# Attention scores of an encoder block: the products with the queries' lo parts in half the array's rows, side by side, with the stages of a unit in another order

## The chip, the core and the metric

The kernel runs on one core of a Trainium2 chip. The metric is the device time of one execution in microseconds; the time before is the median of three runs. The engines are named as in the profile: PE (TensorE, matrix multiplication; PEld is its loading of weights), DVE (VectorE), ACT (ScalarE), POOL (GpSimd), SP (SyncE, which here only issues transfers).

## What is computed

One encoder block on 2048 positions of 1024 channels in float32: an input projection, four heads of differential attention beside Fourier mixing, an output projection, a gated MLP with a convolution of width three, and norms. The change concerns attention. Each head has two components of queries and keys (64 channels each) and one set of values (128 channels):

```
s = jnp.einsum('bqhcd,bkhcd->bhcqk', qi, k) * scale
s = s - slopes[None, :, None, None, None] * dist[None, None, None]
p = jax.nn.softmax(s, axis=-1)
a = p[:, :, 0] - lam * p[:, :, 1]
return jnp.einsum('bhqk,bkhv->bqhv', a.astype(v.dtype), v)
```

The index `c` is the component, and `dist` the distance of the two positions. The output of a head is then normalized (its scale goes into the output projection).

## The kernel before

**Precision.** The matmuls' operands have the type float32r. Each is split (`split`, lines 77 to 87) into a hi part, a copy converted to float32r (ACT), and a lo part, the difference (DVE mostly). A product is the sum of three matmuls, hi by hi, hi by lo and lo by hi (`mm3`, lines 119 to 128).

**Where queries and keys come from.** `in_proj` writes them, split, to DRAM: `qd` and `kd` are indexed by head, component, hi or lo, channel (64) and position (lines 272 to 275). Queries carry the factor of the scores already.

**A unit of attention** is one head and one block of 128 queries, so there are 4 x 16 = 64 units, heads outside. The loop of lines 657 to 686 goes in steps, four to a unit; `t` counts them, and step `t` serves several units at different stages:

- `scores(n, c, half)`, lines 543 to 577: the scores of unit n for component c against 1024 keys, one call a step. The 64 channels of a component leave half of PE's 128 rows over, so the keys' hi and lo parts are stacked: a key tile has, for each component, hi in partitions 0 to 63 and lo in 64 to 127 (`load_k`). The query tile holds four blocks (component, hi or lo), each one twice, in the upper and the lower 64 partitions (`load_q`). So a matmul with the hi query gives hi by hi plus hi by lo, and one with the lo query gives lo by hi plus lo by lo: two matmuls for each 512 keys, four a call, 16 a unit, all with 128 rows (line 567). They go into a PSUM tile `s` of 128 x 1024; there are two of these. A DVE pass (line 572) adds the distances, writes the result to the unit's tile `z` and keeps a running minimum. After the second half, ACT computes the exponential of the 128 x 2048 tile and its sum (line 576).
- `combine(n, half)`, lines 579 to 589: DVE makes the coefficient of the second component from the two sums (lines 583 and 585); POOL, with ACT for a quarter of the columns, scales the second component by it (`scale_half`, lines 439 to 444) and POOL adds it to the first (line 589).
- `transposes(n, g)`, lines 591 to 600: two units later, four of the 16 key blocks a step are transposed on PE into one of two PSUM tiles `pt` (line 598), and split into the tile `at` by ACT (hi, line 81) and DVE (lo, line 82).
- `values(pr, kbs)`, lines 602 to 609: products with the values for a pair of units, two key blocks a step, six matmuls of 256 columns, into a PSUM tile `o`.
- `finish(pr, stage)`, lines 611 to 632: squares and copy out of PSUM on ACT, sums of squares on PE (line 624), and the norm's scale in four small POOL instructions (lines 628 and 630 to 632).

In the loop, a unit n issues in its own four steps the scores of component 0 in steps 0 and 1 and of component 1 in steps 2 and 3, with the exponentials at steps 1 and 3; the first half of combine comes in step 3 and the second in step 0 of the next unit. `zp` has three tiles `z` for each component.

**What orders the work.** Each engine works through a queue in order. The queues' order comes from the framework in which the kernel is written: it takes the order of issue as a priority and moves instructions by a model of when they are ready, so a queue can differ from the order of the code. Loads of queries, keys and values are issued from POOL: two issues for a query tile of 512 positions (line 504, every four units) and two for a head's keys (line 458).

**Around it.** The first units of attention are issued among the last steps of the Fourier mixing (`fourier`); the output projection follows.

Of the kernel before, what the change touches and what calls it, by code (L numbers as in the profile page):

```python
# [20 lines left out]
P = 128  # L21
D = 1024
S = 2048
NB = S // P
KB = D // P
H = 4
DH = 64
# [3 lines left out]
HALF = 512  # L31
# [4 lines left out]
SLOPES = [2.0 ** (-8.0 * (h + 1) / H) for h in range(H)]  # L36
# [4 lines left out]
class Block:  # L41
# [96 lines left out]
    def in_proj(self, es_u, es_f):  # L138
        nc, a = self.nc, self.a
        up = self.pool(es_u, "u", 1, side="right")  # L140
        self.up = up
        with ExitStack() as es, ExitStack() as es01:
# [47 lines left out]
            with ExitStack() as esn:  # L190
# [15 lines left out]
                for _ in range(20):  # L206
                    r = nc.tensor.transpose(busy[:, :P], self.ident, self.ident)
# [3 lines left out]
                u = [up.tile([P, HALF], F32, tag="u", bufs=18, name=f"u{n}") for n in range(NB)]  # L211
                r = {}
# [37 lines left out]
            for blk, b, gs in ((1, 0, range(4)), (1, 1, range(4)), (0, 0, (0, 1)), (0, 1, (0, 1)),  # L250
                               (0, 1, (2,)), (0, 0, (2, 3)), (0, 1, (3,))):
                dst = self.kd if blk else self.qd
                if (blk, b, gs) == (0, 1, (2,)):
                    es01.close()
                    self.fourier_operands(es_f, pst)
                else:
                    wt = weights(blk * HALF + b * W)
                for g in gs:
                    row = p.tile([P, HALF], F32, tag="row", name=f"row{blk}{b}{g}")
                    nc.sync.dma_start(row, self.rsd[g * HALF:(g + 1) * HALF].partition_broadcast(P))  # L260
                    for hh in range(2):
                        h, cs = 2 * b + hh, slice(hh * P, hh * P + P)
                        ps = pso.tile([P, HALF], F32, tag="o", name=f"pz{blk}_{h}_{g}")
                        self.mm3(ps, [(wt[kb][:, 0, cs], wt[kb][:, 1, cs], hth[g][:, kb, :], htl[g][:, kb, :])
                                      for kb in range(KB)])
                        st = p.tile([P, 2, HALF], F32R, tag="zst", name=f"zst{blk}_{h}_{g}")
                        z = p.tile([P, HALF], F32, tag="z", bufs=1, name=f"z{blk}_{h}_{g}")
                        nc.vector.scalar_tensor_tensor(
                            z, ps, 1.0 if blk else -1.0 / (math.sqrt(DH) * SLOPES[h]),
                            row, ALU.mult, ALU.mult)  # L270
                        self.split(z, st[:, 0, :], st[:, 1, :])
                        for c in range(2):
                            (nc.scalar if blk or gs[-1] < 3 else nc.sync).dma_start(
                                dst[h, c, :, :, g * HALF:(g + 1) * HALF].rearrange("l d t -> d l t").bitcast(F32),
                                st[c * DH:(c + 1) * DH].bitcast(F32))


# [176 lines left out]

    def load_k(self, h):
        t = self.slot(self.K_SLOT[h], [2, S], f"k{h}")
        for c in range(2):
            self.nc.gpsimd.dma_start(t[:, c], self.kd[h, c].rearrange("l d t -> (l d) t"))
        return t

    def load_v(self, h, behind=None):
# [37 lines left out]
        nc.vector.tensor_scalar(self.neglam, self.neglam, -LAMBDA_INIT, None, ALU.add)  # L499

    def load_q(self, h, n, behind=None):
        qt = self.kp.tile([P, 4, HALF], F32R, tag="q", name=f"q{h}_{n}")
        for r in range(2):
            load = self.nc.gpsimd.dma_start(
                qt[r * DH:(r + 1) * DH],
                self.qd[h].rearrange("c l d t -> d (c l) t")[:, :, n * HALF:(n + 1) * HALF])
            if behind is not None:
                self.issue_after(load, behind, True)
        return qt
# [21 lines left out]
    def attention(self, pss):  # L531

        nc, a = self.nc, self.a
        with ExitStack() as es:
# [5 lines left out]
            ks, vs, qs = {0: self.k0}, {}, {(0, 0): self.q0}  # L540
            zs, sums, recips, ats, pos = {}, {}, {}, {}, {}

            def scores(n, c, half):
                h, i = units[n]
                if c == 0 and half == 0:
                    if i % 4 == 2 and n + 2 < NU:
                        h2, i2 = units[n + 2]
                        qs[h2, i2 // 4] = self.load_q(h2, i2 // 4, self.ot_done[2] if n == 2 else None)
                    if n == 1:
                        vs[0] = self.load_v(0, self.ot_done[1])  # L550
                    kind, head = self.KV_AT.get(n, (None, None))
                    if kind == "k":
                        ks[head] = self.load_k(head)
                    if kind == "v":
                        vs[head] = self.load_v(head)
                    sums[n] = (sp.tile([P, 4], F32, tag="mn", name=f"mn{n}"), sp.tile([P, 2], F32, tag="ss", name=f"ss{n}"))
                    if n % 2 == 0:
                        recips[n // 2] = sp.tile([P, 2, 2], F32, tag="rr", name=f"rr{n}")
                mn, ss = sums[n]
                if half == 0:  # L560
                    zs[n, c] = zp.tile([P, S], F32, tag=f"z{c}", name=f"z{n}_{c}")
                zt, qt, kt = zs[n, c], qs[h, i // 4], ks[h]
                ps = pss.tile([P, 1024], F32, tag="s", name=f"s{n}_{c}{half}")
                for l in range(2):
                    for j in range(2):
                        k0 = half * 1024 + j * HALF
                        nc.tensor.matmul(ps[:, j * HALF:(j + 1) * HALF], qt[:, 2 * c + l, i % 4 * P:i % 4 * P + P],  # L567
                                         kt[:, c, k0:k0 + HALF], start=l == 0, stop=l == 1)
                d0 = (NB - 1 - i) * P + half * 1024
                m0 = c * 2 + half  # L570

                nc.vector.tensor_tensor_reduce(  # L572
                    zt[:, half * 1024:(half + 1) * 1024], ps, dist[:, d0:d0 + 1024], SLOPES[h],
                    3.0e38 if half == 0 else mn[:, m0 - 1:m0], ALU.add, ALU.min, mn[:, m0:m0 + 1])
                if half == 1:
                    nc.scalar.activation(zt, zt, AF.Exp, bias=mn[:, 2 * c + 1:2 * c + 2], scale=-1.0,  # L576
                                         accum_out=ss[:, c:c + 1])
# [79 lines left out]
            for t in range(4 * (NU + LAG + 4)):  # L657
                if t < 4 * LAG:
                    yield
                elif t == 4 * LAG:  # L660
# [7 lines left out]
                n, c, half = t // 4, t // 2 % 2, t % 2  # L668
                if n < NU:
                    scores(n, c, half)  # L670
                for args in steps.get(t, ()):
                    if args not in loading:
                        loading[args] = self.out_weights(wp, *args)
# [2 lines left out]
                for stage, lag in enumerate((8, 10)):  # L676
                    if v >= lag and (v - lag) % 8 == 0 and (v - lag) // 8 < NU // 2:
                        finish((v - lag) // 8, stage)
                if n < NU and t % 4 == 3:
                    combine(n, 0)  # L680
                if 0 <= n - LAG < NU:
                    transposes(n - LAG, t % 4)
                if 0 <= n - 1 < NU and t % 4 == 0:
                    combine(n - 1, 1)
                if 0 <= v < 8 * (NU // 2):
                    values(v // 8, [v % 8 * 2, v % 8 * 2 + 1])
# [463 lines left out]
```

## Time and profile before

| | us |
| --- | --- |
| median of three runs | 2571.42 (2570.17 to 2577.55) |
| the profiled execution's own time | 2574.7 |
| its span, first to last instruction | 2572.9 |
| attention: first and last score matmul start at | 410.3 and 954.8 |

The mean clock that PE was granted in the profiled execution was 0.992 of full speed. In the rows of the profile "L567" is line 567 of the kernel; `s<-k,q` reads "writes tile s, reads tiles k and q"; `x4` counts instructions that are shown together. A row of the chain of waits has the start, the length and the engine with tile and line. A row of the timeline has the start, the length from the first start to the last end, the engine, and in brackets how long the engine had been idle and what ended that. Matmuls are pipelined: the length shown for one is longer than the time from its start to the next one's.

### The profile page before, as it was taken

What the parts mean: (1) busy time and instruction counts of PE and PEld (TensorE: products, weight loads), DVE (VectorE), ACT (ScalarE), POOL (GpSimd) and SP (SyncE); (2) the same over time, 40 slices, a digit from 0 to 9 for tenths busy, and PEclk for the clock granted to TensorE, in tenths of its full rate; (3) what the DMA queues carried; (4) which work ended last, traced back from release to release, by engine and by line L of the source; (5) the groups of instructions that cost most, each with busy time, mean ns of one, the idle gap of its engine ahead of it and who ended that gap; (6) DMA issues with size and microseconds to landing.
All of it is one profiled execution on the core that took longest, in us unless ns stands there. A gap on an engine that the chain in (4) does not pass through costs nothing.

```text
span 2572.9 us, 34950 instructions
## 1 busy us (share of the span) xinstructions
PE 2516.6 (98%) x13021; PEld 2114.6 (82%) x13021; DVE 1752.6 (68%) x2691; ACT 1301.9 (51%) x2036; POOL 716.9 (28%) x797
## 2 busy tenths in 40 slices
PE   9999999999999999978999999999999999999998
PEld 9998877888888888866888888877888888888886
DVE  4533358988889996786877777657777777434443
ACT  6321246888888883233544454444454445333332
POOL 1300015888988883271010010000000000000000
PEclk9999999999999999988999999999999999999999
DMA  8335558343332205554222221454212222546463
GB/s 264 98 125 139 152 143 237 66 74 73 74 75 50 48 26 173 181 174 140 107 74 79 88 79 70 160 181 155 91 74 76 88 83 85 185 137 219 146 204 113
DMA packets 146154, 309.12 MB, mean 120 GB/s; under 512 B 12080, under 2 KB 69440, under 8 KB 138816
## 3 DMA queue, kind: packets, MB, share of 16 engines
q1 hardware_dynamic: 90816, 226.60, 26.2%
q0 software_dynamic: 18256, 34.57, 6.7%
q10 hardware_dynamic: 36912, 45.72, 5.8%
q8 instruction: 102, 1.67, 0.3%
q14 instruction: 68, 0.56, 0.1%
HBM read 225.05 MB, written 81.80 MB: 119 GB/s over the span
## 4 chain that ended last, share of the span: by engine, by line
PE 87%; DVE 5%; DMA 4%; issue 1%; POOL 1%; ACT 1%; SPq 0%; POOLq 0%; ACTq 0%; DVEq 0%
PE s L567 9%; PE pd L127 5%; PE pd L125 5%; PE pd L126 5%; PE pt L598 4%; PE o L125 3%; PE o L127 3%; PE o L126 3%; PE pz L125 2%; PE pz L127 2%; PE pz L126 2%; DMA hb<-htd 2%; PE pv L127 1%; PE pv L126 1%; PE pv L125 1%
## 5 line engine op out<-in xcount | busy, mean ns | idle before, releaser
L589 POOL TENSOR_TENSOR z<-z,z 128x1024 f32<-128x1024 f32 x128 | 307.1, 2414 | 0.1
L82 DVE TENSOR_TENSOR d<-wd,d 128x512 fp32r<-128x512 f32 x240 | 157.0, 689 | 211.7 <-ACT d L81 211.4
L567 PE MATMUL s<-k,q 128*128 128x512 f32 x1024 | 281.5, 396 | 3.0 <-DVE mn L572 2.0
L576 ACT ACTIVATE z<-z,mn 128x2048 f32<-128x2048 f32 x128 | 257.5, 2012 | 33.7 <-DVE mn L572 32.7
L81 ACT ACTIVATE d<-wd 128x512 fp32r<-128x512 f32 x240 | 141.8, 626 | 236.9 <-PE pd L127 186.2
L125 PE MATMUL pd<-d,d 128*128 128x512 f32 x640 | 251.8, 393 | 1.9 <-ACT d L81 1.4
L127 PE MATMUL pd<-d,d 128*128 128x512 f32 x640 | 251.2, 393 | 0.5 <-DVE d L82 0.5
L126 PE MATMUL pd<-d,d 128*128 128x512 f32 x640 | 251.5, 393 | 0.0
L567 PEld LDWEIGHTS s<-k,q 128*128 128x128 f32 x1024 | 174.5, 188 | 29.4 <-DVE mn L572 5.0
L572 DVE CUSTOM_DVE_ANT_0 z<-s,dist,mn 128x1024 f32<-128x1024 f32 x128 | 163.8, 1280 | 38.6 <-PE s L567 37.8
L82 DVE TENSOR_TENSOR at<-pt,at 128x512 fp32r<-128x512 f32 x256 | 169.9, 686 | 8.5 <-ACT at L81 8.4
L81 ACT ACTIVATE at<-pt 128x512 fp32r<-128x512 f32 x256 | 147.5, 592 | 48.2 <-PE pt L598 44.8
L125 PE MATMUL o<-at,v 128*128 128x256 f32 x512 | 162.0, 316 | 0.0
L598 PE MATMUL pt<-ident,z 128*128 128x128 f32 x1024 | 156.7, 276 | 5.1 <-DVE at L82 5.1
L572 DVE CUSTOM_DVE_ANT_0 z<-s,dist 128x1024 f32<-128x1024 f32 x128 | 155.8, 1217 | 5.4 <-PE s L567 4.4
L598 PEld LDWEIGHTS pt<-ident,z 128*128 128x128 f32 x1024 | 125.7, 144 | 36.3 <-issue 10.5
L98 POOL TENSOR_SCALAR y_rs<-y_rs 128x1 f32<-128x1 f32 x16 | 6.9, 429 | 524.9 <-ACT sq L95 524.9
L126 PE MATMUL o<-at,v 128*128 128x256 f32 x512 | 146.3, 286 | 0.0
L125 PEld LDWEIGHTS pd<-d,d 128*128 128x128 f32 x640 | 120.1, 188 | 30.6 <-ACT d L81 1.8
L127 PEld LDWEIGHTS pd<-d,d 128*128 128x128 f32 x640 | 120.1, 188 | 29.0 <-DVE d L82 1.4
L127 PE MATMUL o<-at,v 128*128 128x256 f32 x512 | 143.7, 281 | 0.0
L126 PEld LDWEIGHTS pd<-d,d 128*128 128x128 f32 x640 | 120.1, 188 | 27.7 <-DVE d L82 0.3
(1058 smaller groups left out, 6895.0 us busy)
## 6 DMA issues: line engine op xcount, KB each, us to landing
wu<-in_w_up SPq DMA_DIRECT2D x44, 1024.0 KB, 4.8
wd<-in_w_down SPq DMA_DIRECT2D x88, 512.0 KB, 3.6
wd<-gd SPq DMA_DIRECT2D x88, 256.0 KB, 3.9
q<-qd POOLq DMA_DIRECT2D x32, 512.0 KB, 7.0
gd<-t SPq DMA_DIRECT2D x22, 512.5 KB, 2.6
gd<-t SPq DMA_DIRECT2D x22, 511.5 KB, 3.1
wst<-in_w_in SPq DMA_DIRECT2D x72, 128.0 KB, 3.6
xt<-in_xt SPq DMA_DIRECT2D x16, 512.0 KB, 4.6
```

Of the source, the lines that this page charges most:

```text
L81: r = nc.scalar.activation(hi, src, AF.Copy)
L82: return r, (lo_engine or nc.vector).tensor_tensor(lo, src, hi.bitcast(F32), ALU.subtract)
L98: nc.gpsimd.tensor_scalar(t[:, 1:2], t[:, 0:1], 1.0 / D, EPS, ALU.mult, ALU.add)
L125: mm(ah, bh, start=first and i == 0, stop=False)
L126: mm(ah, bl, start=False, stop=False)
L127: r = mm(al, bh, start=False, stop=last and i == n - 1)
L567: nc.tensor.matmul(ps[:, j * HALF:(j + 1) * HALF], qt[:, 2 * c + l, i % 4 * P:i % 4 * P + P], kt[:, c, k0:k0 + HALF], start=l == 0, stop=l ...
L572: nc.vector.tensor_tensor_reduce(zt[:, half * 1024:(half + 1) * 1024], ps, dist[:, d0:d0 + 1024], SLOPES[h], 3.0e38 if half == 0 else mn[: ...
L576: nc.scalar.activation(zt, zt, AF.Exp, bias=mn[:, 2 * c + 1:2 * c + 2], scale=-1.0, accum_out=ss[:, c:c + 1])
L589: nc.gpsimd.tensor_tensor(z[:, x], z[:, x], z1[:, x], ALU.add)
L598: nc.tensor.transpose(pt[:, j * P:(j + 1) * P], zs[n, 0][:, kb * P:(kb + 1) * P], self.ident)
```

## The change

The third product pair, lo query by keys, no longer uses the whole array. Hi queries are multiplied as before with stacked hi and lo keys (128 rows). Lo queries are multiplied by hi keys alone, 64 rows: component 0 in partitions 0 to 63, component 1 in partitions 64 to 127, issued in turn, into different PSUM tiles. The product lo by lo is no longer computed. For this the keys of component 1 are stacked the other way round (lo above, hi below), so `load_k` issues three transfers a head. The query tile has three blocks instead of four (hi of each component, twice, and one block with the lo parts of component 0 above component 1), in three transfers; `qd` is indexed by hi or lo before component, so that the lo parts lie together.

One call of `scores` now makes a half (1024 keys) for both components, eight matmuls into both `s` tiles, in steps 0 and 2; the DVE passes of both follow. The exponentials are a function of their own, at steps 2 and 3, behind that step's transposes; both halves of `combine` come in step 1 of the next unit.

```diff
-                                dst[h, c, :, :, g * HALF:(g + 1) * HALF].rearrange("l d t -> d l t").bitcast(F32),
+                                d[:, :, g * HALF:(g + 1) * HALF].rearrange("l d t -> d l t").bitcast(F32),
...
     def load_k(self, h):
         t = self.slot(self.K_SLOT[h], [2, S], f"k{h}")
-        for c in range(2):
-            self.nc.gpsimd.dma_start(t[:, c], self.kd[h, c].rearrange("l d t -> (l d) t"))
+        self.nc.gpsimd.dma_start(t[:, 0], self.kd[h, 0].rearrange("l d t -> (l d) t"))
+        for l in range(2):
+            self.nc.gpsimd.dma_start(t[(1 - l) * DH:(2 - l) * DH, 1], self.kd[h, 1, l])
...
     def load_q(self, h, n, behind=None):
-        qt = self.kp.tile([P, 4, HALF], F32R, tag="q", name=f"q{h}_{n}")
-        for r in range(2):
-            load = self.nc.gpsimd.dma_start(
-                qt[r * DH:(r + 1) * DH],
-                self.qd[h].rearrange("c l d t -> d (c l) t")[:, :, n * HALF:(n + 1) * HALF])
+        qt = self.kp.tile([P, 3, HALF], F32R, tag="q", name=f"q{h}_{n}")
+        c = slice(n * HALF, (n + 1) * HALF)
+        loads = [(qt[r * DH:(r + 1) * DH, :2], self.qd[h, 0, :, :, c].rearrange("c d t -> d c t")) for r in range(2)]
+        for o, i in loads + [(qt[:, 2], self.qd[h, 1, :, :, c].rearrange("c d t -> (c d) t"))]:
+            load = self.nc.gpsimd.dma_start(o, i)
...
-            def scores(n, c, half):
+            def scores(n, half):
...
+                ps = [pss.tile([P, 1024], F32, tag="s", name=f"s{n}_{c}{half}") for c in range(2)]
+                out = lambda c, j: ps[c][:, j * HALF:(j + 1) * HALF]
+                for c in range(2):
+                    for j in range(2):
+                        nc.tensor.matmul(out(c, j), qt[:, c, u], kt[:, c, cols[j]], start=True, stop=False)
+                for j in range(2):
+                    for c in range(2):
+                        r = slice(c * DH, (c + 1) * DH)
+                        nc.tensor.matmul(out(c, j), qt[r, 2, u], kt[r, c, cols[j]], start=False, stop=True)
+                d0 = (NB - 1 - i) * P + half * 1024
+                for c in range(2):
+                    m0 = c * 2 + half
+                    nc.vector.tensor_tensor_reduce(
+                        zs[n, c][:, half * 1024:(half + 1) * 1024], ps[c], dist[:, d0:d0 + 1024], SLOPES[h],
+                        3.0e38 if half == 0 else mn[:, m0 - 1:m0], ALU.add, ALU.min, mn[:, m0:m0 + 1])
+
+            def exps(n, c):
                 mn, ss = sums[n]
...
-                for l in range(2):
-                    for j in range(2):
-                        k0 = half * 1024 + j * HALF
-                        nc.tensor.matmul(ps[:, j * HALF:(j + 1) * HALF], qt[:, 2 * c + l, i % 4 * P:i % 4 * P + P],
-                                         kt[:, c, k0:k0 + HALF], start=l == 0, stop=l == 1)
...
-                if n < NU:
-                    scores(n, c, half)
+                n = t // 4
+                if n < NU and t % 2 == 0:
+                    scores(n, t // 2 % 2)
...
-                if n < NU and t % 4 == 3:
-                    combine(n, 0)
                 if 0 <= n - LAG < NU:
                     transposes(n - LAG, t % 4)
-                if 0 <= n - 1 < NU and t % 4 == 0:
+                if n < NU and t % 4 > 1:
+                    exps(n, t % 4 - 2)
+                if 0 <= n - 1 < NU and t % 4 == 1:
+                    combine(n - 1, 0)
                     combine(n - 1, 1)
```

More of the change, by code (lines that the diff above doesn't have):

```diff
@@ L272, in in_proj @@
                         for c in range(2):
+                            d = dst[h, c] if blk else dst[h, :, c]
                             (nc.scalar if blk or gs[-1] < 3 else nc.sync).dma_start(
-                                dst[h, c, :, :, g * HALF:(g + 1) * HALF].rearrange("l d t -> d l t").bitcast(F32),
+                                d[:, :, g * HALF:(g + 1) * HALF].rearrange("l d t -> d l t").bitcast(F32),
                                 st[c * DH:(c + 1) * DH].bitcast(F32))
@@ L541, in attention @@
             zs, sums, recips, ats, pos = {}, {}, {}, {}, {}
-            def scores(n, c, half):
+            def scores(n, half):
                 h, i = units[n]
-                if c == 0 and half == 0:
+                if half == 0:
                     if i % 4 == 2 and n + 2 < NU:
@@ L558, in scores @@
                         recips[n // 2] = sp.tile([P, 2, 2], F32, tag="rr", name=f"rr{n}")
-                mn, ss = sums[n]
[L560 to L563, printed above, removed]
-                for l in range(2):
-                    for j in range(2):
-                        k0 = half * 1024 + j * HALF
-                        nc.tensor.matmul(ps[:, j * HALF:(j + 1) * HALF], qt[:, 2 * c + l, i % 4 * P:i % 4 * P + P],
-                                         kt[:, c, k0:k0 + HALF], start=l == 0, stop=l == 1)
@@ L569, in scores @@
[L569 to L577, printed above, removed]
+                    for c in range(2):
+                        zs[n, c] = zp.tile([P, S], F32, tag=f"z{c}", name=f"z{n}_{c}")
@@ new lines, in scores @@
+                mn = sums[n][0]
+                qt, kt = qs[h, i // 4], ks[h]
+                u = slice(i % 4 * P, i % 4 * P + P)
+                cols = [slice(half * 1024 + j * HALF, half * 1024 + (j + 1) * HALF) for j in range(2)]
+                ps = [pss.tile([P, 1024], F32, tag="s", name=f"s{n}_{c}{half}") for c in range(2)]
[3 more added lines that the diff above has]
+                        nc.tensor.matmul(out(c, j), qt[:, c, u], kt[:, c, cols[j]], start=True, stop=False)
@@ new lines, in scores @@
+                for j in range(2):
[3 more added lines that the diff above has]
+                d0 = (NB - 1 - i) * P + half * 1024
+                for c in range(2):
+                    m0 = c * 2 + half
+                    nc.vector.tensor_tensor_reduce(
+                        zs[n, c][:, half * 1024:(half + 1) * 1024], ps[c], dist[:, d0:d0 + 1024], SLOPES[h],
+                        3.0e38 if half == 0 else mn[:, m0 - 1:m0], ALU.add, ALU.min, mn[:, m0:m0 + 1])
@@ L579, in combine @@
+            def exps(n, c):
+                mn, ss = sums[n]
+                nc.scalar.activation(zs[n, c], zs[n, c], AF.Exp, bias=mn[:, 2 * c + 1:2 * c + 2], scale=-1.0,
+                                     accum_out=ss[:, c:c + 1])
             def combine(n, half):
@@ L667, in attention @@
                     pso = self.pool(es, "at_po", 2, PSUM)
-                n, c, half = t // 4, t // 2 % 2, t % 2
-                if n < NU:
-                    scores(n, c, half)
+                n = t // 4
+                if n < NU and t % 2 == 0:
+                    scores(n, t // 2 % 2)
                 for args in steps.get(t, ()):
```

## The prediction

> **What bounds the kernel now.** I read the page first, for the shares and the chain that ended last, then the busy time of the engines over one pair of units, then the chain inside that pair, then each engine's own queue there. The page:
>
> ```profile
> PE 2516.6 (98%) x13021; PEld 2114.6 (82%) x13021; DVE 1752.6 (68%) x2691; ACT 1301.9 (51%) x2036; POOL 716.9 (28%) x797
> ...
> PE 87%; DVE 5%; DMA 4%; issue 1%; POOL 1%; ACT 1%; SPq 0%; POOLq 0%; ACTq 0%; DVEq 0%
> ```
>
> PE (TensorE) is busy all the time and carries 87% of the chain, but these are averages over stages. The change touches attention alone, so I read that stage. The chain there, first and last regular scores and one stretch between:
>
> ```profile
> 444.78 0.93 PE s L567 x4
> ...
> 954.30 0.95 PE s L567 x4
> ```
>
> ```profile
> 649.85 0.92 PE s L567 x4
> 650.77 0.44 PE pt L598 x4
> 651.21 0.12 PE o L125
> 651.33 0.12 PE o L126
> ...
> 651.91 0.94 PE s L567 x4
> ```
>
> ```profile
> 666.92 0.93 PE s L567 x4
> ```
>
> One step is four score matmuls (0.93), four transposes (0.44) and six value matmuls (six times 0.12, 0.70), 2.07 us in all, with nothing between them. Eight steps, a pair of units, last 666.92 - 649.85 = 17.07 us, so a unit takes 8.53 us; eight times 2.07 is 16.56, and most of the rest goes to the finishing stage's matmuls (line 624). From 444.78 to 954.30 there are 509.5 / 8.53 = 59.7 units; I count 59.5, for a few small holes. What the other engines do in that pair (columns: length, then busy time of PE, weight loads, DVE, ACT, POOL, each with its count):
>
> ```profile
> 649.85:666.92 17.07, 17.07 (x117) 15.22 (x117) 15.18 (x32) 14.45 (x21) 15.02 (x14) 1.00 0.43 70
> ```
>
> PE is the bound, at full clock (1.00), but three engines are within 12 to 15% of it. This is the row that matters most: PE can give back only about a tenth before another engine is late.
>
> **The change part by part.**
>
> *The matmuls.* Every score matmul before uses the whole array. Per unit there are 16, 512 columns each; afterwards 8 whole ones and 8 of 64 rows, which are to run two at a time. One costs 0.93 / 4 = 0.235 us. If two half-row matmuls take the time of one, a unit saves 4 x 0.235 = 0.94 us; if they run one after the other it saves nothing. It cannot save more, since each still streams 512 columns. No row of before shows a matmul of fewer than 128 rows, so both ends stay. I take the full overlap: the two of a pair read different partitions, use different rows, and write different PSUM tiles, and nothing in the program orders one behind the other. The weight loads stay 16 a unit; the value matmuls above have one load each at 0.12 us, so two loads fit into the 0.235 us of a pair, just. By the Trainium skill (TensorE: Matmul & The Clock Gate, Part 3) matmuls in different row groups start some 4 ns apart, and four of 32 rows gained 3.07 times; no run here shows it yet.
>
> *The switch between whole and half rows.* Each half of a unit goes to half rows and back, four switches a unit. Nearest rows: scores to transposes costs nothing (649.85 + 0.92 = 650.77), transposes to values costs a little:
>
> ```profile
> 653.04 0.37 PE L125 MATMUL o<-at,v 128*128 128x256 f32 x1
> 653.25 0.28 PE L126 MATMUL o<-at,v 128*128 128x256 f32 x1
> 653.37 0.28 PE L127 MATMUL o<-at,v 128*128 128x256 f32 x1
> ```
>
> The first value matmul is followed after 0.21 instead of 0.12 us, so 0.09. The far end is a full wait for the matmul in flight:
>
> ```profile
> L567 PE MATMUL s<-k,q x1024: 387/395/499, 410.3 to 954.8; 128*128 128x512 f32 x171
> ```
>
> It lasts 0.395 where the next starts after 0.235, a tail of 0.16 us. So a switch costs 0 to 0.16 us, a unit 0 to 0.64; I take 0.05 a switch, 0.2 a unit, near the two cheap rows. PE's unit is then 8.53 - 0.94 + 0.2 = 7.8 us, with 7.6 and 8.25 as ends. The Trainium skill (TensorEngine Tiling (Array Packing), Key Properties) says that changing the tiling mode drains the engine. By that rule the upper end holds, and it is the third case below.
>
> *The other queues.* Their work hardly changes, so each one's own sum is a floor. DVE and ACT:
>
> ```profile
> 650.20 0.69 DVE L82 TENSOR_TENSOR at<-pt,at 128x512 fp32r<-128x512 f32 x1
> 650.81 1.28 DVE L572 CUSTOM_DVE_ANT_0 z<-s,dist,mn 128x1024 f32<-128x1024 f32 x1
> 652.02 0.09 DVE L572 DVE_READ_ACCUMULATOR2_ANT mn<- 128x1 f32 x1
> 652.02 0.69 DVE L82 TENSOR_TENSOR at<-pt,at 128x512 fp32r<-128x512 f32 x1
> 652.89 1.23 DVE L572 CUSTOM_DVE_ANT_0 z<-s,dist 128x1024 f32<-128x1024 f32 x1 [0.19 <-PE s L567]
> 654.04 0.08 DVE L572 DVE_READ_ACCUMULATOR2_ANT mn<- 128x1 f32 x1
> 654.96 1.28 DVE L572 CUSTOM_DVE_ANT_0 z<-s,dist,mn 128x1024 f32<-128x1024 f32 x1 [0.84 <-PE s L567]
> ```
>
> ```profile
> 649.60 0.57 ACT L81 ACTIVATE at<-pt 128x512 fp32r<-128x512 f32 x1
> 650.38 0.72 ACT L443 ACTIVATE z<-z,cf 128x512 f32<-128x512 f32 x1 [0.21 <-DVE cf L585]
> 651.24 0.60 ACT L81 ACTIVATE at<-pt 128x512 fp32r<-128x512 f32 x1
> 652.20 2.01 ACT L576 ACTIVATE z<-z,mn 128x2048 f32<-128x2048 f32 x1 [0.35 <-DVE mn L572]
> 654.12 0.18 ACT L576 ACTIVATION_READ_ACCUMULATOR z<-z,mn 128x1 f32 x1
> 654.21 0.57 ACT L81 ACTIVATE at<-pt 128x512 fp32r<-128x512 f32 x1
> ```
>
> From start to next start a score pass on DVE takes 1.15 (652.89 to 654.04) or 1.21 us (650.81 to 652.02), a lo split 0.6 (650.20 to 650.81): per unit 2 x 1.15 + 2 x 1.21 + 4 x 0.6 = 7.1, and with the reciprocal and its kin about 7.5 (the window's 15.18 / 2 is 7.6). ACT: 14.45 / 2 = 7.2, of which two exponentials at 2.01 each. POOL also issues the loads:
>
> ```profile
> 649.34 1.31 POOL L504 DMA_DIRECT2D q<-qd  x2
> 650.68 1.13 POOL L441 TENSOR_SCALAR z<-z,cf 128x1024 f32<-128x1024 f32 x1
> 651.78 0.19 POOL L630 TENSOR_SCALAR ft<-ft 128x2 f32<-128x2 f32 x1
> ...
> 654.97 0.71 POOL L631 TENSOR_TENSOR ft<-ft,mhalf 128x2 f32<-128x2 f32 x1
> ...
> 658.02 0.18 POOL L632 TENSOR_TENSOR fs<-ft,rr 128x2 f32<-128x2 f32 x1
> 658.18 0.19 POOL L628 TENSOR_TENSOR f<-rr 128x2 f32<-128x2 f32 x1
> 659.95 1.13 POOL L441 TENSOR_SCALAR z<-z,cf 128x1024 f32<-128x1024 f32 x1 [1.58 <-DVE cf L585]
> 661.05 0.69 POOL L444 TENSOR_SCALAR z<-z,cf 128x512 f32<-128x512 f32 x1
> 661.71 4.78 POOL L589 TENSOR_TENSOR z<-z,z 128x1024 f32<-128x1024 f32 x2
> ```
>
> A combine is 1.1 + 0.67 + 4.75 = 6.5 us, the norm 0.19 + 0.71 + 0.18 + 0.19 = 1.3 a pair, 0.65 a unit. A query load is two issues, 1.31 us, every four units; three issues afterwards, 1.95 if each costs the same; no row gives a price by size. That is 0.49 instead of 0.33 a unit. Keys go from two issues to three a head, at the same price 0.65 us in 16 units; with them and the values I add 0.1. POOL's floor becomes 6.5 + 0.65 + 0.49 + 0.1 = 7.75 us, a little above DVE's 7.5 and beside PE's 7.8. So even if everything ran packed, a unit would take about 7.75.
>
> *The stages reordered.* Now both components' score tiles of a half are filled in one step and both exponentials come ready together, instead of half a unit apart. I walk through it from the end (time 0) of the second half's scores, in the order in which the code issues; the engines' queues are sorted by a planner with costs of its own (before, ACT's queue above has hi, scale, hi, exponential, where the code issues hi, hi, scale, exponential), so this is an estimate from the rows above. With full overlap PE ends the next scores after two steps' transposes and values, 2 x 1.14, and 0.94 + 0.47, at 3.7. DVE does two passes and a lo split, to about 3.0. The first exponential starts at 1.15 + 0.18 = 1.3 (DVE's accumulator row at 652.02 to ACT's at 652.20) and holds ACT until 3.3; the transposes of the unit's last step end at about 1.6, so their hi copy waits and ends at 3.85, and the lo split behind it runs from 3.95 to 4.55: DVE stood idle for almost 1 us. Its next two passes run to 6.9 instead of 6.05. The second exponential holds ACT until 5.9, two hi copies follow to 7.0, DVE's lo splits to 8.1, and the coefficients may come ahead of the next pass too. PE meanwhile waits for the second score tile, which DVE frees at 6.9, and ends the next half at 7.85. So a unit closes at 8.1 to 8.4: DVE, held up by ACT, has taken PE's place. The planner may place a hi copy ahead of the first exponential, which pulls it towards the floor of 7.75. I take 8.2 us.
>
> *The rest.* Both halves of combine now stand one behind the other on POOL, two steps later for the first half. Ready coefficients come at about 6.2 of the walk, the first half 3.5 later, at 9.7, and the transposes that read it stand in PE's queue at about 3.7 + 8.2 = 11.9: covered, with about 2 us of slack; a query load of 1.95 in between uses it up. Two more issues ahead of the distance table at the start are 1.3 us at most, beside Fourier work. The stores of q and k keep number and size. The end of attention waits for two exponentials in a row, 1 us more. I cost these at 0 to 3 us together, and take 0.
>
> **The sum.** 59.5 units x (8.53 - 8.2) = 20 us. The profiled execution took 2574.7 (span 2572.9 and 1.8 around it), so 2554.7 against that one; the median of the three runs, 2571.42, is 3.3 lower: 2551. A difference of 0.3%, 7.7 us, is about what a measurement can tell from none.
>
> **The rivals.**
>
> *Near the floor.* The planner sorts ACT well and a unit takes 7.75 to 8.0. For it: in this pair all three helpers have over 1 us of slack a unit. Against: all four engines would be over 90% busy at once, and there are two score tiles only. 59.5 x 0.65 = 39 us less: about 2532. Chance 0.18.
>
> *Each switch drains.* PE at 8.25, and with the walk's stalls, where a wait of PE on the second score tile is no longer made up, about 8.5: 2570, no change. Chance 0.17. It is the skill's drain rule; the cheap change at 649.85 to 650.77 speaks against so high a price, though it is another kind of change.
>
> *Half-row matmuls do not overlap.* Then the change does not do what it says: PE keeps 8.53 and pays the switches, at 0.09 each 0.36 a unit: 8.9, and 59.5 x 0.36 = 21 us more, 2593. With 0.16 a switch it would be 2609. A unit has four pairs and four switches, so PE loses from the point where a pair costs more than 0.47 less one switch: with 0.09, from 0.38. Nothing in the profile speaks against it, since no row has such a matmul. Chance 0.25.
>
> **How the numbers follow.** The forecast, 2551, has 0.40 (its own range 2537 to 2566). Faster: it and the floor, 0.58; no change: the drain, 0.17; slower: 0.25. The range leaves out the best part of the floor case (below 2526) and the dearer switches (above 2594): about 2 in 10.
>
> **What would show it.** Half-row rows in the profile (64 rows of the array) at starts in pairs, a pair in about 0.24 us, and a half's scores in 1.4 to 1.5 us. A window of a pair of units of about 16.4 us instead of 17.07, PE no longer busy throughout, DVE and ACT at about 90%. Between 560 and 950 us the waits are now (total, times, longest):
>
> ```profile
> DVE z L572 <- PE s L567: 33.3, 62, 0.9
> ...
> DVE at L82 <- ACT at L81: 4.4, 19, 0.2
> ```
>
> DVE waits for PE; afterwards its lo splits should wait for ACT by tens of us, and score matmuls for DVE's passes. If PE stays at 100% of a longer pair, switches or missing overlap are the cause; if a transposition waits for POOL, its floor was set too low.

## The result, and the profile after

The time rose. The median is 2671.75 us (2666.95 to 2673.7, four runs) against 2570.8 for the kernel before beside it: a ratio of 1.0385, 95% interval 1.0362 to 1.0409, so 101 us more. The profiled execution took 2671.89 us (span 2670.1), 97 us more than the one shown of before. The forecast was 20 us less. One run of `e15_passes`, 10984 us, counts as slow and is in none of the ratios below.

The page, busy time and the chain of waits by engine:

```profile
PE 2586.3 (97%) x13021; PEld 2073.0 (78%) x13021; DVE 1760.9 (66%) x2691; ACT 1302.4 (49%) x2036; POOL 728.8 (27%) x817
...
PE 79%; DVE 7%; POOL 6%; DMA 5%; issue 3%; ACT 1%; SPq 0%; POOLq 0%; ACTq 0%; DVEq 0%
```

Two things are new at once. PE is busy for 70 us more, although a quarter of its score time was to go, and POOL has 6% of the chain instead of 1%. The groups by line show the place: the first score pass of DVE for each component, before and then after (count, shortest, median and longest length in ns, start of the first and the last):

```profile
L572 DVE CUSTOM_DVE_ANT_0 z<-s,dist x128: 1204/1216/1240, 411.9 to 953.4; 128x1024 f32<-128x1024 f32 x128
```

```profile
L583 DVE CUSTOM_DVE_ANT_0 z<-s,dist x128: 1200/1222/1256, 416.8 to 1049.6; 128x1024 f32<-128x1024 f32 x128
```

Attention starts 4.9 us later and lasts 632.8 instead of 541.5 us, 91.3 more; together 96 of the 97. Below, "a unit" is the time from DVE's first pass of unit 8 to that of unit 60, by 52: 8.55 us before, 10.23 after. Two units in the windows (length, then busy time of PE, weight loads, DVE, ACT, POOL):

```profile
699.29:719.47 20.18, 19.16 (x119) 13.70 (x118) 15.28 (x30) 14.60 (x21) 14.29 (x13) 1.00 0.03 9
```

DVE, ACT and POOL work as long as before (15.18, 14.45 and 15.02), so none of them became the bound. PE is busy for 9.6 us a unit at full clock, and 1.0 us in two units it stands still. What PE does with a half, in the chain of waits (start, length; L574 has the whole array, L578 half its rows):

```profile
706.00 0.48 PE s L574 x2
706.48 0.43 PE s L578
706.91 0.66 PE s L574 x2
707.58 0.66 PE s L578 x3
708.23 0.59 PE pt L611 x4
```

The code issues four whole and then two pairs of half-row matmuls. PE's queue has two whole, one half-row, two whole, three half-row: the planner put the parts of component 0 ahead. That is four switches a half, and one pair instead of two. Of the 128 halves 88 run like this one; 24 have two whole and two half-row matmuls twice, four switches and no pair, and 16 have the order in which the code issues. Here scores and transposes take 2.82 us, where before two steps' scores and one step's transposes took 2 x 0.93 + 0.44 = 2.30.

And where PE stands still, in the timeline (ACT, DVE, POOL and PE by turns; in brackets the idle time and what ended it):

```profile
713.81 0.19 ACT L589 ACTIVATION_READ_ACCUMULATOR z<-z,mn 128x1 f32 x1
```

```profile
717.04 0.15 DVE L596 RECIPROCAL rr<-ss 128x2 f32<-128x2 f32 x1
717.81 1.28 DVE L583 CUSTOM_DVE_ANT_0 z<-s,dist,mn 128x1024 f32<-128x1024 f32 x1 [0.62 <-PE s L578]
719.02 0.08 DVE L583 DVE_READ_ACCUMULATOR2_ANT mn<- 128x1 f32 x1
719.02 0.27 DVE L598 TENSOR_SCALAR cf<-ss,neglam,rr 128x1 f32<-128x1 f32 x1
```

```profile
719.47 1.12 POOL L442 TENSOR_SCALAR z<-z,cf 128x1024 f32<-128x1024 f32 x1 [1.99 <-DVE cf L598]
720.57 0.69 POOL L445 TENSOR_SCALAR z<-z,cf 128x512 f32<-128x512 f32 x1
721.23 4.74 POOL L602 TENSOR_TENSOR z<-z,z 128x1024 f32<-128x1024 f32 x2
```

```profile
723.65 0.65 PE L611 MATMUL pt<-ident,z 128*128 128x128 f32 x4 [1.00 <-POOL z L602]
```

A unit's sums are complete at 714.0, when ACT has its second exponential. The coefficient made of them comes only at 719.02: the last thing ahead of it in DVE's queue is a score pass of the next unit, and that pass waits for PE (0.62 us). POOL waits for the coefficient (1.99), then the transposes for POOL (1.00).

### The profile page after: what moved, and what is told of

Same layout as the page of the kernel before. It is cut to its first block, busy times and chain, and to the rows that moved or that the text cites. A ratio compares the mean times of both kernels' runs of the same rounds, so it can differ in the third digit from the quotient of the medians.

```text
span 2670.1 us, 34950 instructions
## 1 busy us (share of the span) xinstructions
PE 2586.3 (97%) x13021; PEld 2073.0 (78%) x13021; DVE 1760.9 (66%) x2691; ACT 1302.4 (49%) x2036; POOL 728.8 (27%) x817
## 4 chain that ended last, share of the span: by engine, by line
PE 79%; DVE 7%; POOL 6%; DMA 5%; issue 3%; ACT 1%; SPq 0%; POOLq 0%; ACTq 0%; DVEq 0%
PE pd L125 4%; PE pd L127 4%; PE pd L126 4%; PE s L574 4%; PE pt L611 4%; PE s L578 4%; POOL z L602 3%; PE o L125 2%; PE o L127 2%; PE o L126 2%; PE pz L125 2%; PE pz L127 2%; PE pz L126 2%; DVE z L583 2%; DMA hb<-htd 2%
## 5 line engine op out<-in xcount | busy, mean ns | idle before, releaser
L574 PE MATMUL s<-k,q 128*128 128x512 f32 x512 | 175.0, 427 | 1.0 <-DVE mn L583 0.8
L611 PEld LDWEIGHTS pt<-ident,z 128*128 128x128 f32 x1024 | 116.5, 143 | 75.7 <-POOL z L602 48.9
L578 PE MATMUL s<-k,q 64*128 64x512 f32 x512 | 156.5, 465 | 0.0
```

Source lines behind the costliest of these rows:

```text
L574: nc.tensor.matmul(out(c, j), qt[:, c, u], kt[:, c, cols[j]], start=True, stop=False)
L578: nc.tensor.matmul(out(c, j), qt[r, 2, u], kt[r, c, cols[j]], start=False, stop=True)
L611: nc.tensor.transpose(pt[:, j * P:(j + 1) * P], zs[n, 0][:, kb * P:(kb + 1) * P], self.ident)
```

## The experiments

Theory 1 (A in the expectations): the order of PE's score matmuls costs the time (switches, lost pairs). Theory 2 (B): the stages' order does, through the coefficient. Rivals were that half-row matmuls do not overlap, and that the additional transfers cost the time. All kernels (ratio and interval against the kernel before, run on the same chip):

| kernel | what | median us | ratio (95%) | unit us |
| --- | --- | --- | --- | --- |
| after | the change | 2671.75 | 1.0385 (1.0362 to 1.0409) | 10.23 |
| e1_order | half-row pairs in the written order | 2672.88 | 1.0396 (1.0377 to 1.0416) | 10.13 |
| e2_whole | stages reordered, whole array | 2624.13 | 1.0198 (1.0181 to 1.0215) | 9.37 |
| e4_stages | half rows, exps and combine at before's places | 2638.66 (one run) | | 9.42 |
| e5_both | e4 and e1 | 2644.5 | 1.0283 (1.0268 to 1.0299) | 9.69 |
| e8_coef | after, coefficient earlier | 2631.21 | 1.0229 (1.0214 to 1.0244) | 9.42 |
| e6_order_coef | e1, coefficient earlier | 2604.7 | 1.0129 (1.0113 to 1.0144) | 8.95 |
| e7_whole_coef | e2, coefficient earlier | 2593.31 | 1.0086 (1.0068 to 1.0103) | 8.88 |
| e9_serial_coef | e6, queue c0 c0 c1 c1 | 2612.99 (one run) | | 9.10 |
| e10_same_rows | e6, all half-row matmuls in the same 64 rows | 2642.84 (one run) | | 9.52 |
| e11_before_pairs | before's stages, one pair a step | 2616.19 | 1.0175 (1.0158 to 1.0192) | 9.05 |
| e12_component | a component in every second step, two pairs | 2594.62 | 1.0092 (1.0077 to 1.0107) | 8.70 |
| e13_store | e12 with before's two key transfers | 2578.67 | 1.0024 (1.0015 to 1.0034) | 8.61 |
| e14_component_whole | e13, whole array | 2586.37 | 1.0066 (1.0045 to 1.0087) | 8.74 |
| e15_passes | e13, DVE's two passes together | 2571.64 | 0.9999 (0.9990 to 1.0008) | 8.47 |
| e16_passes | e15, also lo splits ahead of the next passes | 2597.11 | 1.0097 (1.0084 to 1.0110) | 8.89 |

Slower than every range expected of them came out e1, e5, e12 and e16; e4, e6, e13, e14 and e15 fell between or just beside theirs.

**The written order alone.** `e1_order` chains the eight matmuls of a half, and nothing else:

```diff
+                for f, c, j in ((whole, 0, 0), (whole, 0, 1), (whole, 1, 0), (whole, 1, 1), (rows, 0, 0), (rows, 1, 0), (rows, 0, 1), (rows, 1, 1)):
+                    mm = f(c, j)
+                    if last is not None:
+                        self.issue_after(mm, last)
+                    last = mm
```

> The changed kernel with PE's queue held to the written order: four whole-array score matmuls, then the four half-row ones with the two components in turn, so two switches a half and two adjacent pairs, where the changed kernel's queue has four switches and one pair. From the starts in its trace a half's scores should fall from 2.3-2.4 to about 1.7 us. Theory A (the switches on PE are the whole loss): PE then has about 8.3 us of work a unit, and the time is 2550 to 2590. Theory B (the loop set by the reordered stages: coefficient behind the next unit's second-half pass on DVE, then POOL, then the transposes): a unit falls only by the scores' part of that loop, to about 9.5 us, so the time is about 2630.

The time did not move, 2672.88: theory 1 alone falls. But PE's own work did get shorter (busy 2526.7 us instead of 2586.3), and waits took its place. The chain of waits, one turn and the end of the one before it:

```profile
705.25 0.71 PE s L576 x4
705.95 1.27 DVE z L588
707.24 0.20 DVE cf L603
...
707.62 1.07 issue
708.69 0.70 POOL z L445
709.39 2.34 POOL z L607
...
711.78 0.66 PE pt L616 x4
...
714.98 0.47 PE s L572 x2
715.45 0.71 PE s L576 x4
716.15 1.27 DVE z L588
717.44 0.20 DVE cf L603
```

From coefficient to coefficient, 707.24 to 717.44, are 10.20 us, about the unit ("issue" is time in which an engine waited for nothing that the profile shows; here it is that of POOL's first scale). It is a loop: coefficient, POOL's scales and first sum, transposes, then the next scores behind them in PE's queue, DVE's pass of these scores, and behind that pass the next coefficient. Whatever PE saves in it is spent waiting for POOL (waits of e1 between 560 and 950 us: total, times, longest):

```profile
PEld pt L616 <- POOL z L607: 63.0, 31, 2.4
POOL z L442 <- DVE cf L603: 58.5, 33, 3.5
PE pt L616 <- POOL z L607: 49.5, 31, 2.0
```

**The stages alone, and the coefficient.** `e2_whole` keeps the reordered stages, with all score matmuls, loads and tiles as before:

```diff
-                        r = slice(c * DH, (c + 1) * DH)
-                        nc.tensor.matmul(out(c, j), qt[r, 2, u], kt[r, c, cols[j]], start=False, stop=True)
+                        for j in range(2):
+                            nc.tensor.matmul(out(c, j), qt[:, 2 * c + l, u], kt[:, c, cols[j]], start=l == 0, stop=l == 1)
```
 `e8_coef`, `e6_order_coef` and `e7_whole_coef` put the second-half passes of a unit behind the coefficient of the unit before in DVE's queue, on top of after, e1 and e2:

```diff
-                    nc.vector.tensor_tensor_reduce(
+                    r = nc.vector.tensor_tensor_reduce(
...
+                    if half == 1 and n > 0:
+                        self.issue_after(r, coef[n - 1])
```

> The reordered stages alone: scores of both components in one step, exponentials and combine at the new places, but all score matmuls with 128 rows as before, with the loads and tiles of before (lo by lo is computed again). Theory A: no half rows, no switches, so the time of before within 10 us, 2560 to 2580. Theory B: DVE's queue has the coefficient behind the second-half pass in every second unit, so the loop holds there; a unit of 9.0 to 9.5 us, 2600 to 2630.

> The changed kernel with the coefficient held ahead of the second-half passes and PE's queue left to the planner, which switches between whole and half rows four times a half. PE's own work is then about 9.4 us a unit (2.3 us of scores a half), and this binds: 2620 to 2640. If switches did not matter it would equal the run with the written order.

> PE's queue in the written order, and on DVE the coefficient of a unit held ahead of the next unit's second-half passes (it stood between the two). Theory B (the loop coefficient, POOL, transposes, scores, pass): POOL starts about 1.4 us earlier, the transposes' wait for it falls from 1.5-1.7 us a unit to about 0.2, and with PE's own 8.4 us a unit takes 8.5 to 8.8: 2570 to 2590. The rival, that half-row matmuls cost this time by themselves: no change from 2673.

> Whole-array score matmuls with the reordered stages (the 2624 us kernel) and the coefficient held ahead of the second-half passes. Theory B: the loop no longer binds, PE's 8.53 us does: 2575 to 2595. Against the run with half rows in written order and the same coefficient this gives what half rows are worth in themselves: by the starts in the trace 0.1 to 0.2 us a half saved, so half rows 0 to 20 us the faster.

Reordering the stages alone costs 2624.1 - 2571.0 = 53 us; with the coefficient moved, 2593.3 - 2572.2 = 21. With half rows the same move takes the 101 us to 2631.2 - 2572.2 = 59, 42 less, and the written order then takes these to 2604.7 - 2572.2 = 32.5. With the written order the same move takes 69 us, from 2672.9 - 2571.0 = 102 to 32.5. So both theories hold, but in this order: the loop first, and only without it does PE's order count, for 26.5 us where it counted for none. In `e8_coef` PE's queue mixes whole and half rows much as in the change (54 of the 128 halves like the one shown there, 35 without a pair, 39 in the written order; so the planner's order moved too, and part of the 42 us may be due to that), and it fills the chain of 700 to 722 us by itself:

```profile
by line: PE s L574 24.6%; PE s L578 23.8%; PE pt L613 17.7%; PE o L125 11.6%; PE o L127 10.7%; PE o L126 10.7%; PE o L639 2.4%; issue 0.1%
```

**Undoing the stages halfway.** `e4_stages` and `e5_both` put the exponentials ahead of the transposes and combine's halves back to steps 3 and 0, with both components' scores still made together:

```diff
+                if n < NU and t % 4 > 1:
+                    exps(n, t % 4 - 2)
...
+                if n < NU and t % 4 == 3:
+                    combine(n, 0)
...
-                if 0 <= n - 1 < NU and t % 4 == 1:
-                    combine(n - 1, 0)
+                if 0 <= n - 1 < NU and t % 4 == 0:
                     combine(n - 1, 1)
```

> The half-row matmuls with the exponentials and the halves of combine issued where before has them (first half of combine in step 3, second in step 0 of the next unit); PE's order left to the planner, which mixes whole and half rows. Theory A: switches as many as in the changed kernel, so about its time, 2640 to 2680. Theory B: the coefficient stands ahead of the next unit's second-half passes, POOL is no longer late, and the unit falls to PE's own work, about 9.2 us: about 2610, and no waits of transposes for POOL.

> Both: PE's queue in the written order for the eight score matmuls, and exponentials and combine issued where before has them. Theory A and B both expect the best time of the four here; A the same as with the order alone (2550 to 2590), B better than with the order alone by about 1 us a unit: 2555 to 2580 against about 2630.

At 2638.7 and 2644.5 they help by about 30 us, less than the coefficient's place alone; in `e5_both` ACT's exponentials have 18.6% of the chain of 700 to 722 us, and POOL waits 64.8 us for the coefficient between 560 and 940 (36.4 in before). Issuing the coefficient where before issues it did not bring it to POOL in time.

**Do half rows overlap?** `e10_same_rows` is e6 with the half-row matmuls of both components in the upper 64 rows (component 1 then multiplies other parts); `e9_serial_coef` is e6 with the half-row matmuls of component 0 queued ahead of those of component 1. The edit of e10, and the end of e9's list:

```diff
-                    r = slice(c * DH, (c + 1) * DH)
+                    r = slice(0, DH)
...
+                ... (rows, 0, 0), (rows, 0, 1), (rows, 1, 0), (rows, 1, 1)):
```

> As the run with the written order and the coefficient ahead, but all four half-row matmuls of a half use the upper 64 rows, for both components (component 1 thus multiplies other parts, its scores are not the reference's). If the pairs ran together because they lie in different rows, their starts, 0.003 us apart there, move to 0.235 to 0.33 us apart, a unit is 0.9 to 1.3 us longer on PE, and the time goes from 2605 to 2640-2670. If a pair's second matmul cost nothing for another reason, the time stays.

> As the run with the written order and the coefficient ahead, but the four half-row matmuls in the order component 0, 0, 1, 1, so that the two that share rows are neighbours in three of the three places but one. Where neighbours in different rows run together, this loses overlap: one more half-row time a half, 0.23 to 0.33 us, up to 0.66 if the one remaining change of rows does not overlap either; a unit 0.5 to 1.3 us longer, 2600 to 2660. If half rows never overlapped, the time would be the same.

Four half-row matmuls in the chain of waits, in e6, e10 and e9:

```profile
704.32 0.46 PE s L572 x2
704.78 0.66 PE s L576 x4
```

```profile
700.63 1.12 PE s L576 x4
```

```profile
718.99 0.67 PE s L576 x4
```

In the same rows they take 1.12 us, in different rows 0.66: the difference, 0.46, is two matmuls of 0.23. Pairs overlap in full, and the rival that they do not falls. Without overlap the kernel takes 2642.8 (one run) instead of 2604.7.

**What an excursion into half rows costs.** `e11_before_pairs` has before's stages, and in each step two whole matmuls and one pair for the two 512-key blocks, whose keys are stacked in opposite order (eight transfers of keys a head; lo by lo is left out, as in the change). `e12_component` makes all 2048 keys of one component in every second step, four whole and two pairs, with the exponential behind them. `e13_store` has the keys stored in stacked order, so that two transfers a head do; `e14_component_whole` is that kernel with the whole array (`r = slice(0, P)`, keys stored as before). The matmul of e12 and e13 (e11 has the same with its one tile `ps`), their place in the loop, and the store of e13 (`blk` is true for keys):

```diff
+                            r = slice(j * DH, (j + 1) * DH) if l else slice(0, P)
+                            mm = nc.tensor.matmul(ps[f][:, j * HALF:(j + 1) * HALF], qt[r, 2 * c + l, u],
+                                                  kt[r, c, k0:k0 + HALF], start=l == 0, stop=l == 1)
...
-                if n < NU:
+                if n < NU and half == 0:
                     scores(n, c, half)
...
-                        self.split(z, st[:, 0, :], st[:, 1, :])
+                        l = g % 2 if blk else 0
+                        self.split(z, st[:, l, :], st[:, 1 - l, :])
```

> Half rows alone, in the stages of before: each step makes one component's scores of 1024 keys with two whole matmuls and one pair of half-row ones for its two blocks of 512 keys (keys of every second block stacked lo above hi, in eight transfers a head; lo by lo left out). By the starts measured so far a step's scores take 0.23 + 0.327 + 0.003 + 0.325 = 0.885 us, and the first transposes 0.06 more, against 0.93: one pair pays for one excursion into half rows and back. So 2565 to 2580, no change from before. If half rows lost time by themselves as the whole change did, 2600 or more; if switching were nearly free, as predicted, 0.8 us a unit less: 2525.

> The same matmuls, but each second step makes all 2048 keys of one component: four whole matmuls, then two pairs, PE's queue in this order; exponentials and combine where before has them, so the coefficient is early and the exponentials stay half a unit apart. One excursion for two pairs: 0.69 + 0.327 + 0.34 + 0.325 + 0.06 = 1.74 us against 1.87, so a unit 0.26 us less on PE, 8.27. If nothing else binds: 2555 to 2560. If the two score tiles, now filled together, make PE wait for DVE's passes, as in the reordered stages with the coefficient ahead (21 us left over there): 2570 to 2580.

> The kernel of one component a step (4 whole matmuls, then 2 half-row pairs in every second step), but the keys are stored in the order in which they are stacked, so a head's keys come in two transfers again instead of eight. If the late start of the run before (first DVE pass at 423.1 us instead of 411.9) is due to the transfers, the start goes back to 412 to 416 and the time falls by about 10 us, to 2580 to 2588. If the start is later for another reason, the time stays at about 2594. Time for a unit as in the run before, about 8.7 us. Theory 'half rows save too little': still not below the kernel before.

> The same structure with the same two transfers a head, but all eight score matmuls use the whole array. Theory 'two pairs an excursion save about 0.13 us each, 0.26 a unit': if PE binds, 0.26 x 59.5 = 15 us more than with half rows, 2595 to 2603. Rival 'the waits of this order of stages bind, not PE': the same time as with half rows, within 4 us. Rival 'half rows cost more than they save here too': less time than with half rows.

Scores and the transposes behind them in the chains of e11, e13 (the two whole matmuls of its first tile had run at 705.99) and e14:

```profile
703.03 0.90 PE s L574 x4
703.93 0.59 PE pt L608 x4
```

```profile
701.51 1.59 PE s L572 x8
...
706.81 1.13 PE s L572 x6
707.93 0.59 PE pt L605 x4
```

```profile
702.45 1.85 PE s L571 x8
704.30 0.44 PE pt L604 x4
```

Eight whole matmuls take 1.85; with two pairs 1.85 - 0.47 = 1.38 would do, but they take 1.59, and the transposes behind take 0.59 instead of 0.44. An excursion, two switches, costs 0.21 + 0.15 = 0.36 us, and a pair saves 0.235: two pairs gain 0.11, one loses. In e11, 0.90 + 0.59 stands against 0.93 + 0.44, 0.12 more a step and 0.48 a unit, and its unit is 9.05 - 8.55 = 0.50 longer. Half rows in e13 do pay, 7.7 us against e14, about 0.13 a unit where the excursions allow 0.22. Against before nothing is won, since filling both score tiles in one step costs 2586.4 - 2573.0 = 13 us by itself (e14). Storing the keys in stacked order took 18 us off (23.8 over before became 5.7), more than expected: 12 of them until unit 8 (494.3 to 482.4 us), the rest in the units.

**DVE's queue once more.** In `e15_passes` the lo split of the first transposes of a pair of steps stands behind the second pass; in `e16_passes` the second lo split also stands ahead of the next pass (the last two lines).

```diff
+                if passes and g % 2 == 0:
+                    self.issue_after(lo, passes[-1])
...
+                    if f == 0 and los:
+                        self.issue_after(r, los[-1])
```

> The kernel of one component a step with two transfers of keys a head; on VectorE the lo split of the first transposes of a step pair is put behind the second of the two score passes, so that the second score tile comes free 0.6 us earlier. If PE's waits for the score passes (13.5 + 3.1 us between 560 and 940 us, about 20 over attention) keep half rows from paying: 2560 to 2570, below the kernel before for the first time. If the transpositions then wait for their lo split instead: 2576 to 2582, as without it.

> As the last, and the lo split of the second transposes of a step pair is also kept ahead of the next component's passes, so that VectorE's queue is pass, pass, lo, lo throughout. If the waits for passes decide: 2558 to 2570. If the queue, held in this order, makes a pass wait for transposes: 2576 to 2590.

`e15_passes` gains 6 us on e13, counted over the kernel before beside each, and equals that kernel: a unit is 0.085 us shorter than before's, 5 us in all, and the start takes them back (unit 8 at 482.1 instead of 477.8). The gain did not come as expected: PE's waits for the passes are the same 3.1 us in both, and those of its weight loads 13.5 and 14.2,

```profile
PE s L572 <- DVE mn L580: 3.1, 5, 1.4
PE pt L605 <- POOL z L596: 2.1, 2, 1.3
```

```profile
PE s L572 <- DVE mn L580: 3.1, 6, 0.8
```

and what is gone (e13 above, e15 below, 560 to 940 us) is a wait for POOL of 2.1; the rest of the 6 us I cannot place. `e16_passes` shows how tight the queues are: one more order imposed on DVE costs 25 us. No version beat the kernel before.

## Why the prediction was wrong

**The step that failed: "covered, with about 2 us of slack".** The prediction let the coefficients come "at about 6.2 of the walk", supposing that they "may come ahead of the next pass too", and costed the later combine at nothing. In e1, which has the matmuls in the walk's order, the second half's scores of a unit end at 705.96 (705.25 + 0.71 in the chain above). ACT has its second exponential's sum at 712.51, 6.5 us later, so the data were there when the walk had them; the coefficient comes at 717.36, 11.4 after:

```profile
712.32 0.19 ACT L594 ACTIVATION_READ_ACCUMULATOR z<-z,mn 128x1 f32 x1
```

```profile
713.31 0.69 DVE L82 TENSOR_TENSOR at<-pt,at 128x512 fp32r<-128x512 f32 x1
714.95 0.69 DVE L82 TENSOR_TENSOR at<-pt,at 128x512 fp32r<-128x512 f32 x1 [0.95 <-ACT at L81]
...
716.14 1.28 DVE L588 CUSTOM_DVE_ANT_0 z<-s,dist,mn 128x1024 f32<-128x1024 f32 x1 [0.43 <-PE s L576]
...
717.36 0.27 DVE L603 TENSOR_SCALAR cf<-ss,neglam,rr 128x1 f32<-128x1 f32 x1
```

Ahead of it stood two lo splits and a pass of the next unit, with two waits. The walk asked when the data were ready, and not what stood ahead of the coefficient in DVE's queue, though it wrote that the queues are sorted by a planner. The 5 us took the 2 us of slack and closed the loop. Moving the coefficient gives 69 us back with the written order (e1 to e6), 42 without it (after to e8), 32 with the whole array (e2 to e7).

What the walk expected to bind instead, DVE held up by ACT, is hardly seen in the change: between 560 and 950 us DVE's lo splits wait 18.8 us for ACT (4.4 before), and the score matmuls 0.2 us for DVE's passes.

**The order of the matmuls.** The walk gave a half 0.94 + 0.47 us, "in the order in which the code issues". PE's queue split the half rows: in 88 of the 128 halves four switches and one pair. PE's unit became 9.6 instead of 7.8 us, above every case of the prediction; once the loop is gone that is 26.5 us (e8 to e6).

**The switch, "0.05 each, 0.2 a unit".** Measured, 0.36 / 2 = 0.18: three and a half times that, and just above the upper bound of 0.16. The bound counted the tail of the matmul in flight; by the rows of e1 the first weight load behind a switch is not hidden either. Its weight loads and matmuls at one excursion:

```profile
704.50 0.30 PEld L572 LDWEIGHTS s<-k,q 128*128 128x128 f32 x2
705.17 0.30 PEld L576 LDWEIGHTS s<-k,q 64*128 64x128 f32 x4 [0.36 <-issue]
705.84 0.42 PEld L616 LDWEIGHTS pt<-ident,z 128*128 128x128 f32 x4 [0.36 <-issue]
```

```profile
705.17 0.73 PE L576 MATMUL s<-k,q 64*128 64x512 f32 x4
705.84 0.66 PE L616 MATMUL pt<-ident,z 128*128 128x128 f32 x4
```

PEld stands idle for 0.36 us, and the first load of the half rows begins with its matmul at 705.17; so again at 705.84 with the transposes. In these rows none runs ahead across a switch, while the loads of the second pair begin 0.23 us ahead of their matmuls. The records have a whole matmul's start 0.327 us before the first half-row start, 0.09 more than the pitch of 0.235, and the first pair 0.34 before the second, 0.10 more (in e10 too the second half-row matmul comes 0.34 after the first, and the next ones 0.23 apart). Four switches, in the written order, cost 0.72 a unit of the 0.94 won. The Trainium skill's rule that a change of tiling mode drains the engine (TensorEngine Tiling (Array Packing), Key Properties), which the prediction held for the less likely, is borne out in direction by these rows, and the price is higher than its case in the prediction assumed.

**What was right.** The pairs overlap in full and a pair saves 0.235 us. DVE, ACT and POOL do as much as was summed for them, so their floors stand; when a transposition waited for POOL, it was not because "its floor was set too low", as the last sentence had it: POOL was idle, waiting for a coefficient. The rival on the slower side had the sign right and its mechanism wrong.

**The rest of the loss.** With the coefficient early and the written order, 32.5 us are left: 21 are in the reordered stages with the whole array (e7), 11 come with the half rows and their additional transfers, and about 6 of these are lost before unit 8 (487.2 in e6, 480.8 in e7). PE's own work is not longer with half rows: between 640 and 800 us it is busy for 153.5 us in e6 and 156.6 in e7, at 8.95 and 8.88 us a unit, so for 8.59 and 8.69 a unit; the waits are longer. The start had been given "1.3 us at most" for more issues on POOL; the first pass comes 4.9 later. Of the 21, POOL's query loads are a candidate: they wait 16.5 us for PE's scores in e2 and 18.6 in e7 between 560 and 940 us, with combines behind them, and no such wait is among those of before in that window. I did not test it, so how the 21 divide stays open.

## What to carry to other kernels

When a stage is moved, look up what will stand ahead of each of its small instructions in the queue of its engine: a 0.2 us coefficient queued behind a pass that waits for the next unit cost 42 to 69 us here, where half rows without any price for switches would have saved 59.5 x 0.94 = 56. The half-row matmuls overlapped in full (0.66 us for two pairs, 1.12 without overlap), but each excursion out of the whole array and back cost 0.36 us, about one and a half 512-column matmuls, so gather at least two pairs in it (more were not tried), and fix their order by hand where a planner sorts the queue. And before mending one cause, check which one binds: here the better matmul order was worth nothing until the loop was opened, and then 26.5 us.

## What the runs showed of the hardware that was not expected

- Queue order within half rows hardly mattered for the four matmuls: with both of component 0 queued ahead of those of component 1 (e9) they take 0.67 us, as in pairs (0.66), though the whole kernel takes 8 us more (one run). PE seems to have started a matmul of the other rows ahead of one queued before it. The trace does not name the tile of each record, but it shows which matmuls signal another engine, and those are the ones that end a tile, second and fourth as queued; in all 127 such groups of e9 they are the third and fourth to start.
- Part of the price of a switch lies with whatever follows: in the chain of waits four transposes behind half rows take 0.59 us, behind whole matmuls 0.44; in a window of PE's busy time both look like work.
- Eight key transfers a head instead of two go with a first score pass at 423.1 us (e12) instead of 414.4 (e13), 8.7 later, where six more issues at 0.65 us make 3.9. What the rest is was not tried.
